# A decoder layer in one written order: transitions, mixer and attention placed by hand per engine

## The chip, the cores and the metric

One core of a Trainium2 chip runs the whole layer in one launch. The metric is device time in microseconds (us). Engines are called TensorE (PE), VectorE (DVE), ScalarE (ACT), GpSimd (POOL) and SyncE (SP, here only a queue that issues transfers).

## The reference

One layer on x of 256 rows by 2048 columns, float32, with a conditioning vector c:

```
mod = silu(c) @ w_ada + b_ada                      # nine rows of 2048
h = modulate(rms_norm(x, g1), mod0, mod1); x += 0.5 * mod2 * swiglu(h)       # FFN 1, width 5632
h = modulate(rms_norm(x, gm), mod3, mod4)
u, q, k, v, ga, gb = split(h @ w_in)               # 1024, 1024, 128, 128, 2048, 2048 columns
y_pool = multiscale_pool(u) @ w_pool_up            # trailing means over 2, 4, 8, 16 rows
y_attn = window_attention(norm(q), norm(k), v, bias, sinks) @ w_attn_up      # 16 heads, window 128
x += mod5 * ((sigmoid(ga) * y_pool + sigmoid(gb) * y_attn) @ w_o)
h = modulate(rms_norm(x, g2), mod6, mod7); x += 0.5 * mod8 * swiglu(h)       # FFN 2
```

## The kernel before

The 256 rows are two tiles t = 0, 1 of 128 partitions. A `Set` multiplies them with a block of up to 1024 weight columns (`SW`) into four of the eight PSUM banks (two t by two chunks of 512 columns, `CW`); the other four banks take transposes and sums. Each weight row block k (128 rows) is split for precision: ScalarE casts the raw weights to `wh` (L300), VectorE subtracts and leaves `wl` (L304); the rows are split the same way into `hh` and `hl` or, for later stages, `sh` and `sl` (L432, L433). `Set.mm` then makes three products: `hh wh` (L316), `hl wh` (L318), `hh wl` (L320), so a full block of k is 12 matmuls of 128x512. Raw weights come by SP's queue into `RAW` = 6 slots of 1 MB.

Two ways of ordering stand side by side:

- FFN 1 and FFN 2 (`ffn`, and the first stage) are under `tc.manual_schedule()`: each engine runs instructions as they are written. `pushes` loads and splits a block and hands its matmuls to `push`, which emits them `LAG` = 2 blocks later, so splits lie two blocks ahead of TensorE. `at(n, f)` hangs any other step behind the matmuls of push n. `spread` places the adaLN sums (one VectorE multiply-add of 128x1024 per row block of `w_ada`, L253) where the planned VectorE time of a push leaves room under `ROOM`; `will` books such time.
- Everything between (both `transition`s, the projection `w_in`, pooling, attention, merge and the first part of the output projection `w_o`) is written in program order through `run`, with hooks after chosen blocks, and a scheduler orders the engines. AdaLN sums go in by a rate (`ada_side`, L182).

A transition: `tail` runs the last four row blocks of the stage that ends, first for t = 0, then t = 1; after each, `residual` (L456, L457) adds gate times result to x, `sumsq` (L371) squares, `rstd` makes the norm's factor, `scaled` (L392) scales 512 columns, `h_T` (L399) transposes them on TensorE, `h_mod` (L409, L411, L413, L414) modulates and splits. The table of position biases (`toeplitz`, L843, L845) is made at the first transition. At the start of FFN 2 `ffn` takes four SiLUs (L542) ahead of its first weights.

The mixer: `qk_norm` hangs in the pooling projection, `pooling` and `heads` (four heads at a time; logits, bias, softmax) in the first two gate stages, `heads_out` (transposes and product with v) later. After each half of the merged rows, eight columns' blocks are transposed by TensorE (`tr`, `pair_T`, L360) into `mT`, the input of `w_o`. In the FFNs the same turn is made without TensorE: `turn_T` transposes 32x32 blocks on VectorE (L521) and 16 ScalarE moves put them in place (L525).

Of the kernel before, what the change touches and what calls it, by code (L numbers as in the profile page):

```python
# [9 lines left out]
F32 = mybir.dt.float32  # L10
# [25 lines left out]
TAIL = 4  # L36
NS = 7
LAG = 2
ROOM = 2.5
# [3 lines left out]
def trunk_layer(ctx, tc, x, c, w_ada, b_ada, g_ffn1, w_ffn1_gu, w_ffn1_down, g_mix, w_in,  # L43
# [50 lines left out]

    late, plan, pushed, done = deque(), {}, [0], [0]
# [23 lines left out]


# [22 lines left out]
    def acc_sum(b, a):  # L143
        w = a.shape[1]
        hi = t_([P, w], "t2", T2, F32R)
        lo = t_([P, w], "t2", T2, F32R)
        nc.scalar.copy(hi, a)
        nc.vector.tensor_tensor(lo, a, hi.bitcast(F32), ALU.subtract)
        nc.tensor.matmul(b, ones, hi, start=True, stop=False)
        nc.tensor.matmul(b, ones, lo, start=False, stop=True)  # L150

# [16 lines left out]
    def ada_item(j, c0, i, a):  # L168

        if i == 0:  # L170
            a.append(t_([P, SW], "acc", 2))
            if j % 3 == 2:
                nc.gpsimd.memset(a[0], 0.0)
                nc.sync.dma_start(a[0][0:1, :], b_ada[0:1, j * D + c0:j * D + c0 + SW])
        raw = t_([P, 2, SW], "raw", RAW)
        nc.sync.dma_start(raw, ada_v[:, 2 * i:2 * i + 2, j * D + c0:j * D + c0 + SW])
        for k in range(2):
            sc = cs[:, 2 * i + k:2 * i + k + 1]
            if i == k == 0 and j % 3 != 2:
                nc.vector.tensor_scalar_mul(a[0], raw[:, k, :], sc)  # L180
            else:
                nc.vector.scalar_tensor_tensor(out=a[0], in0=raw[:, k, :], scalar=sc, in1=a[0],  # L182
                                               op0=ALU.mult, op1=ALU.add)
        if i < 7:
            return
        for o in range(0, SW, CW):
            b = bank()
            acc_sum(b, a[0][:, o:o + CW])
            if j % 3 == 2:
                if j not in gates:  # L190
                    gates[j] = t_([P, D], "gate", 1)
                nc.scalar.activation(gates[j][:, c0 + o:c0 + o + CW], b, AF.Copy, scale=1.0 if j == 5 else 0.5)
            else:
                mod_col(j, b, c0 + o)

    side, sidec = [], [0, 0]

    def ada_side(js, rate):
        sidec[:] = [0, rate]
        for j, c0 in js:  # L200
            a = []
            side.extend(lambda j=j, c0=c0, i=i, a=a: ada_item(j, c0, i, a) for i in range(8))

    def flush():
        while side:
            side.pop(0)()

    def ada_plan(js, n0):


        where = iter(spread(n0, len(js) * KD, 1.28))

        def sums(j, c0, a, n):
            hl_ = []

            def halves(o):
# [3 lines left out]
                hl_[:] = [hi, lo]  # L220

            def use(o):
                b = bank()
                nc.tensor.matmul(b, ones, hl_[0], start=True, stop=False)  # L224
                nc.tensor.matmul(b, ones, hl_[1], start=False, stop=True)  # L225
                if j % 3 == 2:
                    if j not in gates:
                        gates[j] = t_([P, D], "gate", 1)
                    nc.scalar.activation(gates[j][:, c0 + o:c0 + o + CW], b, AF.Copy, scale=1.0 if j == 5 else 0.5)
                else:  # L230
                    mod_col(j, b, c0 + o)

            for i in range(2):
                at(n + 2 * i, lambda i=i: halves(i * CW))
                at(n + 2 * i + 2, lambda i=i: use(i * CW), True)

        for j, c0 in js:
            a, r = [], []
            for kk in range(KD):
                def go(j=j, c0=c0, kk=kk, a=a, r=r):  # L240
                    if kk == 0:
                        a.append(t_([P, SW], "acc", 2))
                        if j % 3 == 2:
                            nc.gpsimd.memset(a[0], 0.0)
                            nc.gpsimd.dma_start(a[0][0:1, :], b_ada[0:1, j * D + c0:j * D + c0 + SW])
                    if kk % 2 == 0:
                        r[:] = [t_([P, 2, SW], "raw", RAW)]
                        nc.sync.dma_start(r[0], ada_v[:, kk:kk + 2, j * D + c0:j * D + c0 + SW])
# [3 lines left out]
                    else:  # L252
                        nc.vector.scalar_tensor_tensor(out=a[0], in0=r[0][:, kk % 2, :], scalar=sc, in1=a[0],  # L253
                                                       op0=ALU.mult, op1=ALU.add)
                n = next(where)
                at(n, go)
            sums(j, c0, a, n + 1)


    class Set:  # L260
# [27 lines left out]

        def prep(self, k, raw_k, extra=False, fine=False, given=None):
            c0, cw = self.cols  # L290
            if given is not None:
                wh, wl = given, t_([P, cw], "wl", 3, F32R)
            elif extra:
                wx = t_([P, 2, cw], "sg", 1, F32R)
                wh, wl = wx[:, 0, :], wx[:, 1, :]
            else:
                wh = t_([P, cw], "wh", 3, F32R)
                wl = t_([P, cw], "wl", 3, F32R)
# [8 lines left out]
        def mm(self, item, t, chunks=None, k0=0, k1=None):  # L307
# [4 lines left out]
            sl = slice(t * P, (t + 1) * P)  # L312
            ch = [(i, slice(*self.chunks[i])) for i in range(len(self.chunks))]
            ch = [(i, slice(o.start, o.start + o.stop)) for i, o in ch if chunks is None or i in chunks]
            for i, o in ch:
                nc.tensor.matmul(self.banks[t][i], hi[:, sl], wh[:, o], start=first, stop=False)  # L316
            for i, o in ch:
                nc.tensor.matmul(self.banks[t][i], lo[:, sl], wh[:, o], start=False, stop=False)  # L318
            for i, o in ch:
                nc.tensor.matmul(self.banks[t][i], hi[:, sl], wl[:, o], start=False, stop=last)  # L320
# [5 lines left out]
        def pushes(self, ka, kb, k0=0, k1=None):  # L326

            grp = min(2 * SW // self.cols[1], 4)
            for a in range(ka, kb, grp):
                raw = self.load(a, min(grp, kb - a))  # L330
                for k in range(a, min(a + grp, kb)):
                    item = self.prep(k, raw[:, k - a, :])
                    push(lambda item=item: [self.mm(item, t, None, k0, k1) for t in range(T)])

        def step(self, k, raw_k, k0=0, k1=None):
            item = self.prep(k, raw_k)
            for t in range(T):
                self.mm(item, t, None, k0, k1)

    def run(s, hooks=None, k0=0, k1=None):  # L340
        grp = min(2 * SW // s.cols[1], 4)
        k1 = s.nk if k1 is None else k1
        for ka in range(k0, k1, grp):
            n = min(grp, k1 - ka)
            raw = s.load(ka, n)
            for k in range(n):
                s.step(ka + k, raw[:, k, :])
                if hooks and (ka + k) in hooks:
                    hooks[ka + k]()
            sidec[0] += sidec[1]  # L350
            while side and sidec[0] >= 1:
                sidec[0] -= 1
                side.pop(0)()
        return s.banks

    def pair_T(src, f0, dst_fn):
        b = bank()
        for f in range(2):
            for t in range(T):
                nc.tensor.transpose(b[:, (2 * f + t) * P:(2 * f + t + 1) * P], src(t, f0 + f), ident)  # L360
        dst_fn(f0, b)
# [40 lines left out]
    def h_mod(b, n, t, jb, hh, hl, fine=False, fs=range(4)):  # L402
        h = t_([P, 4, P], "t2", T2)
        ks = [(f, 4 * n + f) for f in fs]
        d = lambda k, w: (slice(None), slice(k, k + w), slice(t * P, (t + 1) * P))
        for f, k in ks:
            g_, b_, src = mcol[:, jb + 1, k:k + 1], mcol[:, jb, k:k + 1], b[:, f * P:(f + 1) * P]
            if fine and t == 0 and f % 2 == 0:
                nc.vector.tensor_scalar(h[:, f, :], src, g_, b_, ALU.mult, ALU.add)  # L409
            else:  # L410
                nc.scalar.activation(h[:, f, :], src, AF.Identity, scale=g_, bias=b_)  # L411
            if fine:
                nc.scalar.copy(hh[d(k, 1)], h[:, f:f + 1, :])  # L413
                nc.vector.tensor_tensor(hl[d(k, 1)], h[:, f:f + 1, :], hh[d(k, 1)].bitcast(F32), ALU.subtract)  # L414
        if not fine:
            e = d(4 * n, 4)
            nc.scalar.copy(hh[e], h)
            nc.vector.tensor_tensor(hl[e], h, hh[e].bitcast(F32), ALU.subtract)

    def h_tok(n, t, jb, hh, hl):  # L420
        h_mod(h_T(scaled(n, t)), n, t, jb, hh, hl)
# [5 lines left out]
    def split_stat(src, kept=None):  # L427

        cache = {}
# [6 lines left out]
        def stat(k):  # L436
            ka = k - k % 2
            c = cache if kept is None or not 4 <= k < 4 + KD else kept[2]
            if ka not in c:
                n = min(2, src.shape[1] - ka)  # L440
                if c is cache:
# [6 lines left out]

        return stat
# [15 lines left out]
    def tail(s, c0, jgate, after):  # L465

# [652 lines left out]
```

## Time and profile before

| | |
|---|---|
| time, median of 3 (lowest to highest) | 2023.32 us (2020.91 to 2025.42) |
| the profiled execution's own time, its span | 2025.86 us, 2023.8 us |
| TensorE busy, matmuls | 98%, 8889 |
| VectorE, ScalarE busy | 74%, 54% |
| HBM read | 520 MB, 258 GB/s over the span |
| mean granted TensorE clock | 0.996 |

The profile is of one execution. Rows that begin with a line number group instructions: count, busy us, mean ns of one, then the engine's idle time before them and what ended it.

### The profile page before, as it was taken

What the parts mean: (1) busy time and instruction counts of PE and PEld (TensorE: products, weight loads), DVE (VectorE), ACT (ScalarE), POOL (GpSimd) and SP (SyncE); (2) the same over time, 40 slices, a digit from 0 to 9 for tenths busy, and PEclk for the clock granted to TensorE, in tenths of its full rate; (3) what the DMA queues carried; (4) which work ended last, traced back from release to release, by engine and by line L of the source; (5) the groups of instructions that cost most, each with busy time, mean ns of one, the idle gap of its engine ahead of it and who ended that gap; (6) DMA issues with size and microseconds to landing.
All of it is one profiled execution on the core that took longest, in us unless ns stands there. A gap on an engine that the chain in (4) does not pass through costs nothing. (4 is left out here: it accounts for less than half of the span.)

```text
span 2023.8 us, 23691 instructions
## 1 busy us (share of the span) xinstructions
PE 1985.4 (98%) x8889; PEld 1634.4 (81%) x8889; DVE 1494.3 (74%) x1705; ACT 1083.3 (54%) x1473; POOL 15.0 (1%) x32
## 2 busy tenths in 40 slices
PE   7999999999999998999999999999999999999999
PEld 6788888888788886887788887778888888888887
DVE  6888867988999996868788788758755454565655
ACT  5544457665654455546454455644654645565443
POOL 1000000000000000000000000000000000000000
PEclk9999999999999999999999999999999999999999
DMA  9989745899898984777767887458955555466661
GB/s 363 369 304 336 262 154 188 337 351 356 309 344 337 333 332 165 281 266 241 270 234 286 296 287 268 167 190 328 347 195 191 205 187 188 166 227 209 214 198 68
DMA packets 157778, 523.66 MB, mean 259 GB/s; under 512 B 9525, under 2 KB 23518, under 8 KB 157408
## 3 DMA queue, kind: packets, MB, share of 16 engines
q1 hardware_dynamic: 156992, 521.02, 72.2%
q8 instruction: 69, 1.13, 0.2%
q0 software_dynamic: 672, 1.14, 0.1%
q14 instruction: 45, 0.37, 0.0%
HBM read 520.00 MB, written 2.12 MB: 258 GB/s over the span
## 5 line engine op out<-in xcount | busy, mean ns | idle before, releaser
L304 DVE TENSOR_TENSOR wl<-raw,wh 128x1024 fp32r<-128x1024 f32 (+2 forms) x746 | 844.7, 1137 | 423.1 <-ACT wh L300 419.1
L300 ACT CAST wh<-raw 128x1024 fp32r<-128x1024 f32 (+2 forms) x730 | 728.9, 1002 | 784.5 <-PE bank L318 713.5
L316 PE MATMUL bank<-wh,hh 128*128 128x512 f32 x2072 | 655.2, 391 | 7.5 <-ACT hh L413 4.4
L320 PE MATMUL bank<-wl,hh 128*128 128x512 f32 x2072 | 652.6, 390 | 3.5 <-DVE wl L304 3.2
L318 PE MATMUL bank<-wh,hl 128*128 128x512 f32 x2072 | 652.5, 390 | 0.0
L320 PEld LDWEIGHTS bank<-wl,hh 128*128 128x128 f32 x2072 | 390.0, 189 | 87.6 <-DVE wl L304 7.7
L316 PEld LDWEIGHTS bank<-wh,hh 128*128 128x128 f32 x2072 | 389.2, 189 | 88.5 <-ACT hh L413 5.6
L318 PEld LDWEIGHTS bank<-wh,hl 128*128 128x128 f32 x2072 | 390.5, 189 | 82.2 <-DVE hl L414 0.6
L320 PE MATMUL bank<-wl,sh 128*128 128x512 f32 x692 | 216.0, 390 | 1.8 <-DVE wl L304 1.8
L318 PE MATMUL bank<-wh,sl 128*128 128x512 f32 x692 | 216.3, 389 | 0.0
L316 PE MATMUL bank<-wh,sh 128*128 128x512 f32 x692 | 215.7, 390 | 0.0
L253 DVE SCALAR_TENSOR_TENSOR acc<-raw,cs,acc 128x1024 f32<-128x1024 f32 x139 | 177.7, 1278 | 0.3 <-DMA raw<-in_w_ada_dram 0.3
L320 PEld LDWEIGHTS bank<-wl,sh 128*128 128x128 f32 x692 | 129.7, 188 | 29.0 <-DVE wl L304 2.2
L318 PEld LDWEIGHTS bank<-wh,sl 128*128 128x128 f32 x692 | 129.8, 188 | 27.6 <-DVE sl L433 0.6
L316 PEld LDWEIGHTS bank<-wh,sh 128*128 128x128 f32 x692 | 129.6, 188 | 27.7 <-ACT sh L432 0.5
L525 ACT COPY big<-raw 32x512 f32<-32x512 f32 (+1 forms) x192 | 111.9, 583 | 4.0
L182 DVE SCALAR_TENSOR_TENSOR acc<-raw,cs,acc 128x1024 f32<-128x1024 f32 x77 | 98.5, 1279 | 20.1 <-DMA raw<-in_w_ada_dram 19.6
L631 DVE SCALAR_TENSOR_TENSOR acc<-raw,cs,acc 128x1024 f32<-128x1024 f32 (+2 forms) x74 | 77.6, 1050 | 1.6 <-DMA raw<-in_w_ada_dram 0.7
L433 DVE TENSOR_TENSOR sl<-big,sh 128x512 fp32r<-128x512 f32 x88 | 60.2, 684 | 0.0
L432 ACT CAST sh<-big 128x512 fp32r<-128x512 f32 x88 | 54.3, 617 | 9.7 <-DVE big L948 9.7
L738 DVE TENSOR_TENSOR big<-bank,big 128x512 f32<-128x512 f32 x56 | 36.4, 681 | 0.0
L371 ACT ACTIVATE junk<-x_sb 128x512 bf16<-128x512 f32 x24 | 15.1, 630 | 26.3 <-DVE x_sb L457 24.0
(203 smaller groups left out, 713.4 us busy)
## 6 DMA issues: line engine op xcount, KB each, us to landing
raw<-in_w_ffn_gu_dram SPq DMA_DIRECT2D x175, 1024.0 KB, 4.9
raw<-in_w_ada_dram SPq DMA_DIRECT2D x112, 1024.0 KB, 7.6
raw<-in_w_ffn_down_dram SPq DMA_DIRECT2D x88, 1024.0 KB, 5.8
raw<-in_w_in_dram SPq DMA_DIRECT2D x48, 1024.0 KB, 5.3
raw<-in_w_ada_dram SPq DMA_DIRECT2D x64, 512.0 KB, 7.4
raw<-in_w_o_dram SPq DMA_DIRECT2D x16, 1024.0 KB, 6.1
raw<-in_w_pool_up_dram SPq DMA_DIRECT2D x8, 1024.0 KB, 6.1
raw<-in_w_attn_up_dram SPq DMA_DIRECT2D x8, 1024.0 KB, 6.2
```

The lines of the kernel that those rows point to most:

```text
L182: nc.vector.scalar_tensor_tensor(out=a[0], in0=raw[:, k, :], scalar=sc, in1=a[0], op0=ALU.mult, op1=ALU.add)
L253: nc.vector.scalar_tensor_tensor(out=a[0], in0=r[0][:, kk % 2, :], scalar=sc, in1=a[0], op0=ALU.mult, op1=ALU.add)
L300: nc.scalar.copy(wh, raw_k)
L304: nc.vector.tensor_tensor(wl[:, e], raw_k[:, e], wh[:, e].bitcast(F32), ALU.subtract)
L316: nc.tensor.matmul(self.banks[t][i], hi[:, sl], wh[:, o], start=first, stop=False)
L318: nc.tensor.matmul(self.banks[t][i], lo[:, sl], wh[:, o], start=False, stop=False)
L320: nc.tensor.matmul(self.banks[t][i], hi[:, sl], wl[:, o], start=False, stop=last)
L432: nc.scalar.copy(hi, src[:, k:k + n, :])
L433: nc.vector.tensor_tensor(lo, src[:, k:k + n, :], hi.bitcast(F32), ALU.subtract)
L525: nc.scalar.copy(actT[32 * j:32 * j + 32, k:k + m, :].rearrange("p k (t i r) -> p k t i r", t=T, i=4)[:, :, :, i, :], z[0][32 * i:32 * i + ...
L631: nc.vector.scalar_tensor_tensor(out=acc, in0=r, scalar=sc, in1=acc, op0=ALU.mult, op1=ALU.add)
L738: nc.vector.tensor_tensor(a, b, a, ALU.add)
```

## The change

- The whole kernel is under `manual_schedule`; `run`, `step`, `ada_side` and `tail` go, and everything is placed with `at`.
- `transition`: five last blocks (`TA`) instead of four, their splits in slots of their own (`last_items`), and a written interleave: the first residual runs while the second bank is made; h's halves are written directly from the bank by ScalarE (`direct`); the next stage starts with `hh wh` and `hh wl` and adds `hl wh` later; four blocks (`TB`) of it are prepared ahead. The blocks that follow go through `pushes`.
- Mixer: the stages follow each other as pushes (Q, KV, U, then per half: gate a, pool up, gate b, attention up; then `w_o`). QK norm, pooling and attention are cut into steps one push apart; `with_bank` places a TensorE step at a push and its reader at the next (`hop` avoids a stage's last push). Heads go by two, from pushes 3, 7, 10, 14, 17, 21, 25 and 28 of the first gate stage. Each pair loads its bias on SP's queue into one tile.
- The first half of `mT` is turned by `turn_T` (VectorE, ScalarE), the second still by TensorE.
- The bias table's product goes into FFN 1; its loads, the gains and sinks go to POOL's queue, at the start or in FFN 1. Stores of the last half are issued per bank.
- `ROOM` 2.5 to 2.6; adaLN sums: split, product and use in separate pushes; one block of sums in FFN 1 is cut into two of 512 columns.

The core of the diff:

```diff
+    def hop(n, f, g):
+        while n in ends:
+            n += 1
+        at(n, f)
+        at(n + 1, g)
...
     def transition(s, c0, jgate, jb, nxt):
+        flush()
+        hh, hl = new_h()
+        n = nxt(lambda k: (hh[:, k, :], hl[:, k, :]))
+        items = last_items(s, hh, hl)
+        raw = [n.load(k, 2) for k in range(0, TB, 2)]
...
         for i in range(2):
+            for w in items:
+                s.mm(w, 0, (i,))
+        hi(1, "raw"); lo(1); hi(0, "w"); lo(0)
+        res(0, 0); sumsq(0, col); res(0, 1); sumsq(0, col + 1)
+        rstd(0)
+        x00, x10 = scaled(0, 0), scaled(1, 0)
+        for w in items:
+            s.mm(w, 1, (0,))
+        res(1, 0)
+        for w in items[:3]:
+            s.mm(w, 1, (1,))
+        b00, b10 = h_T(x00), h_T(x10)
+        hi(2, "sg"); lo(2)
+        for w in items[3:]:
+            s.mm(w, 1, (1,))
+        hi(3, "w"); lo(3)
+        m00 = h_mod(b00, 0, 0, jb, hh, hl, True, (2, 3))
+        next(m00)
+        sumsq(1, col); res(1, 1); sumsq(1, col + 1)
+        next(m00, None)
+        rstd(1)
+        for w in nx:
+            n.mm(w, 0, order=(0, 2))
...
+    def with_bank(n, shape, f, g):
+        b = []
+        hop(n, lambda: (b.append(bank(shape)), f(b[0])), lambda: g(b[0]))
...
+        at(n - 1, lambda: nc.sync.dma_start(bias, ...))
         for i in range(2):
+            with_bank(n, (P, TOE), logits(i), add(i))
+        do(n + 2, 1.5, top)
+        at(n + 3, exps)
+        do(n + 4, 1.2, over)
+        for i in range(2):
+            with_bank(n + 5, (P, TOE), turn(i), turned(i))
...
+    for g, n in enumerate((3, 7, 10, 14, 17, 21, 25, 28)):
+        heads(G[0] + n, g)
...
+        if half_ == 0:
+            turn_T(lambda sgb=sgb: sgb[0], 0, SW, mT, lambda t: e + 4 + t, lambda q: e + 7 + q // 2)
```

More of the change, by code (lines that the diff above doesn't have):

```diff
@@ L166, in mod_col, with sums, halves @@
             nc.vector.tensor_tensor(m, m, gcol[:, i * KD + k:i * KD + k + n], ALU.mult)
[L168 to L206, printed above, removed]
     def ada_plan(js, n0):
[L211 to L216, printed above, removed]
+        def sums(j, c0, a, n, o):
+            got = []
+            def halves():
                 hi, lo = t_([P, CW], "t2", T2, F32R), t_([P, CW], "t2", T2, F32R)
@@ L219, in halves, with prod, use @@
                 nc.vector.tensor_tensor(lo, a[0][:, o:o + CW], hi.bitcast(F32), ALU.subtract)
[L220 to L225, printed above, removed]
+                got.extend((hi, lo))
+            def prod():
+                got.append(bank())
+                nc.tensor.matmul(got[2], ones, got[0], start=True, stop=False)
+                nc.tensor.matmul(got[2], ones, got[1], start=False, stop=True)
+            def use():
                 if j % 3 == 2:
@@ L252, in go @@
                     else:
-                        nc.vector.scalar_tensor_tensor(out=a[0], in0=r[0][:, kk % 2, :], scalar=sc, in1=a[0],
+                        nc.vector.scalar_tensor_tensor(out=a[0], in0=r[0][:, kk % nk, :], scalar=sc, in1=a[0],
                                                        op0=ALU.mult, op1=ALU.add)
-                n = next(where)
                 at(n, go)
-            sums(j, c0, a, n + 1)
+                will(n, 1.28 * a_w / SW)
+            n0 = n
+            for i in range(a_w // CW):
+                sums(j, c0, a, n + 1 + 2 * i, i * CW)
     class Set:
@@ L312, in mm @@
             sl = slice(t * P, (t + 1) * P)
+            terms = ((hi, wh), (lo, wh), (hi, wl))
             ch = [(i, slice(*self.chunks[i])) for i in range(len(self.chunks))]
             ch = [(i, slice(o.start, o.start + o.stop)) for i, o in ch if chunks is None or i in chunks]
[L315 to L320, printed above, removed]
+            for q in order:
+                a, w = terms[q]
+                for i, o in ch:
+                    nc.tensor.matmul(self.banks[t][i], a[:, sl], w[:, o], start=first and q == 0, stop=last and q == 2)
         def free(self, t, i):
@@ L332, in pushes @@
                     item = self.prep(k, raw[:, k - a, :])
+                    if between is not None and k == ka:
+                        between()
                     push(lambda item=item: [self.mm(item, t, None, k0, k1) for t in range(T)])
[L335 to L361, printed above, removed]
     ssq = const.tile([P, T, 5], F32, name="ssq")
@@ L461, in sqrt_table @@
         nc.scalar.activation(st[:, 6, 0:1], ssq[:, 1, 1:2], AF.Sqrt)
-    def tail(s, c0, jgate, after):
-        items = []
-        for ka in range(s.nk - TAIL, s.nk, 2):
-            raw = s.load(ka, 2)
-            for k in range(2):
-                items.append(s.prep(ka + k, raw[:, k, :], extra=len(items) == TAIL - 1, fine=True))
-        for i in range(2):
-            for it in items:
-                s.mm(it, 0, (i,))
-        residual(s.banks, c0, jgate, after, (0,))
-        yield
-        for i in range(2):
-            for it in items:
-                s.mm(it, 1, (i,))
-        residual(s.banks, c0, jgate, after, (1,), (0,))
-        yield
-        residual(s.banks, c0, jgate, after, (1,), (1,))
@@ L563, in ffn @@
             if sg is None:
-                s = Set(w_gu, KD, (f0, fw), stat, late=True)
-                s.pushes(0, KD)
+                s, g = g or Set(w_gu, KD, (f0, fw), stat, late=True), None
+                s.pushes(TB + LAG if s.banks else 0, KD)
                 sg = t_([P, T, fw], "sg", 1)
@@ L869, in carve @@
         return a.rearrange("p (a b c) -> p a b c", b=shape[1], c=shape[2])
-    def evac(banks, dst):
-        for t in range(T):
-            for i, b in enumerate(banks[t]):
-                w = b.shape[1]
-                nc.scalar.copy(dst[:, t, i * CW:i * CW + w], b)
-    b, hh, hl = transition(s, SW, 2, 3, lambda stat: Set(WI, KD, (QO, PW), stat, flip=False))
-    big = t_([P, KF * S], "big", 1)
     q_sb = carve(0, T, PW)
@@ new lines, in trunk_layer, with pool_prod, f @@
+    with_bank(nU + 11, (P, CW), k_turn,
+              lambda b: nc.scalar.activation(kT.rearrange("p a b -> p (a b)"), b, AF.Copy, scale=gq[:, 1:2]))
+    with_bank(nU + 12, (P, S), v_turn, lambda b: nc.scalar.copy(vR.rearrange("p a b -> p (a b)"), b))
+    pT_ = []
+    def pool_prod(a):
+        def f(b):
+            if not pT_:
+                pT_.append(t_([P, 8, S], "sg", 1))
+            g = a // 2
+            for f_ in range(2):
+                lhs = lambda t: u_sb[:, t, (a + f_) * P:(a + f_ + 1) * P]
+                nc.tensor.matmul(b[:, f_, :], lhs(0), poolw[:, g, 0:S], start=True, stop=False)
+                nc.tensor.matmul(b[:, f_, P:S], lhs(1), poolw[:, g, S:TOE], start=False, stop=True)
+        return f
@@ new lines, in trunk_layer, with pm_load, mix_prod, f @@
+    pm = []
+    def pm_load():
+        pm.append(t_([P, 8, GW], "raw", RAW))
+        nc.sync.dma_start(pm[0], pool_mix[0].rearrange("g (k p) d -> p (g k) d", p=P))
+    def mix_prod(a):
+        def f(b):
+            g, dd = a // 2, a % 2
+            for k in range(2):
+                nc.tensor.matmul(b, pm[0][:, 2 * g + k, dd * P:(dd + 1) * P], pT_[0][:, 2 * g + k, :],
+                                 start=k == 0, stop=k == 1)
+        return f
+    at(nQ + 4, lambda: nc.sync.dma_start(poolw, pool_w.rearrange("g p n -> p g n")))
@@ new lines, in copies, with sig @@
+    def copies(s, dst, e):
+        for t in range(T):
+            for i, (o, w) in enumerate(s.chunks):
+                at(e + t, lambda t=t, i=i, o=o, w=w: nc.scalar.copy(dst[:, t, o:o + w], s.free(t, i)), True)
+    sQ.pushes(TB + LAG, KD)
+    copies(sQ, q_sb, nK - 1)
+    s = Set(WI, KD, (KO, 256), hstat2, late=True)
+    s.pushes(0, KD)
+    copies(s, kv_sb, nU - 1)
+    s = Set(WI, KD, (UO, PW), hstat2, late=True)
+    s.pushes(0, KD)
+    copies(s, u_sb, G[0] - 1)
+    def sig(s, e, dst):
+        for q, (t, i) in enumerate(tk):
+            at(e + q // 2, lambda t=t, i=i: nc.scalar.activation(dst()[:, t, i * CW:(i + 1) * CW], s.free(t, i), AF.Sigmoid), True)
@@ L1049, in trunk_layer @@
+    s = Set(w_o[0], KD, (0, SW), split_stat(mT), late=True)
+    s.pushes(0, KD)
+    for q, (t, i) in enumerate(tk):
+        at(W1 - 1 + 2 * q, lambda t=t, i=i, s=s: (s.free(t, i), residual(s.banks, 0, 5, lambda *a: None, (t,), (i,))), True)
+        at(W1 + 2 * q, lambda t=t, i=i: sumsq(t, i))
+    at(W1 + 8, sqrt_table)
+    s = Set(w_o[0], KD, (SW, SW), split_stat(mT), late=True)
+    s.pushes(0, KD - TA)
     ov = out[0].rearrange("(t p) d -> p t d", p=P)
     def store(t, n):
-        nc.sync.dma_start(ov[:, t, n * CW:(n + 1) * CW], x_sb[:, t, n * CW:(n + 1) * CW])
@@ L1061, in trunk_layer, with end @@
-    for _ in tail(s, SW, 8, store):
-        pass
+    s = ffn(w_ffn2_gu[0], w_ffn2_down[0], hh, hl, actT, 0, None, g, 8, store, [(8, 0, SW), (8, SW, SW)])
+    flush()
+    items = last_items(s, *new_h())
+    def end(t, a, e):
+        o = slice(SW + a, SW + e)
+        y = t_([P, e - a], "t2", T2)
+        nc.vector.tensor_tensor(y, s.banks[t][a // CW][:, a % CW:a % CW + e - a], gates[8][:, o], ALU.mult)
+        nc.vector.tensor_tensor(x_sb[:, t, o], x_sb[:, t, o], y, ALU.add)
+        nc.sync.dma_start(ov[:, t, o], x_sb[:, t, o])
@@ L1065 @@
+    for t in range(T):
+        for i in range(2):
+            for w in items:
+                s.mm(w, t, (i,))
+            end(t, i * CW, (i + 1) * CW)
 _INS = ['x', 'c', 'w_ada', 'b_ada', 'g_ffn1', 'w_ffn1_gu', 'w_ffn1_down', 'g_mix', 'w_in', 'pool_mix',
```

601 lines of the change are left out of this document (350 added, 251 removed).

## The prediction

> **What bounds the kernel now.** I read the page first, for the share of TensorE and the clock; then the busy time by stretches, which tells stages apart; then TensorE's waits stage by stage; last the order of events in the stretch that loses most.
>
> ```profile
> span 2023.8 us, 23691 instructions
> PE 1985.4 (98%) x8889; PEld 1634.4 (81%) x8889; DVE 1494.3 (74%) x1705; ACT 1083.3 (54%) x1473; POOL 15.0 (1%) x32
> ```
>
> TensorE is the bound: busy for 98% of the span. A busy TensorE need not be at its rate, so the second view counts matmuls per stretch (columns: stretch, length, busy time with the number of instructions of PE, weight loads, VectorE, ScalarE, GpSimd; then the granted clock, the DMA share, GB/s).
>
> ```profile
> core 0: us, PE busy (x) PEld busy (x) DVE busy (x) ACT busy (x) POOL busy (x), PEclk, DMA share, GB/s
> 764.00:800.00 36.00, 29.46 (x128) 22.73 (x127) 23.40 (x51) 19.98 (x46) 0.00 (x0) 0.91 0.54 190
> 800.00:1240.00 440.00, 435.47 (x2066) 359.05 (x2065) 346.49 (x450) 225.99 (x345) 1.44 (x2) 1.00 0.77 269
> 1240.00:1280.00 40.00, 38.25 (x168) 30.82 (x167) 33.43 (x46) 23.38 (x33) 1.44 (x2) 1.00 0.64 223
> 1280.00:1360.00 80.00, 76.00 (x337) 60.77 (x336) 48.49 (x71) 47.53 (x84) 0.00 (x0) 0.98 0.46 161
> 1360.00:2000.00 640.00, 640.00 (x2825) 529.81 (x2824) 379.66 (x363) 338.43 (x408) 2.20 (x4) 1.00 0.63 217
> ```
>
> The last row is the second FFN, whose order is written out by hand already: 2825 matmuls in 640.00 us, 0.2266 us each, TensorE never idle. That is the floor for the other stages. 764 to 800 is the first transition (end of FFN 1, norm, start of the projection), 800 to 1240 the mixer, 1240 to 1280 the output projection, 1280 to 1360 the second transition and the start of FFN 2. TensorE's transposes in the two transitions:
>
> ```profile
> L399 PE MATMUL bank<-ident,t 128*128 128x128 f32 x24 | 3.5, 273 | 3.8 <-DVE t L392 3.8
> L399 PE MATMUL bank<-ident,t 128*128 128x128 f32 x32 | 4.8, 277 | 0.4 <-DVE t L392 0.4
> 787.36 1.03 PE L399 MATMUL bank<-ident,t 128*128 128x128 f32 x8
> ```
>
> Eight in a row end after 1.03 us and one lasts 0.273, so one starts every (1.03 - 0.27)/7 = 0.109 us. Transition 1: 36.00 - 104 x 0.2266 - 24 x 0.109 = 9.8 us lost. Transition 2: 80.00 - 305 x 0.2266 - 32 x 0.109 = 7.4 lost. Output projection: 40.00 - 168 x 0.2266 = 1.9 lost. What TensorE waited for, in the three stretches in turn (us in total, times, longest):
>
> ```profile
> PE bank L399 <- DVE t L392: 3.8, 1, 3.8
> PE bank L316 <- ACT hh L413: 2.7, 2, 2.1
> ...
> PE bank L320 <- DVE wl L304: 2.3, 1, 2.3
> PE bank L945 <- DVE big L984: 0.9, 1, 0.9
> PE bank L150 <- DVE t L148: 0.8, 2, 0.6
> PE bank L980 <- ACT sg L973: 0.4, 1, 0.4
> ...
> PE bank L316 <- ACT wh L300: 1.9, 1, 1.9
> PE bank L320 <- DVE wl L304: 1.8, 1, 1.8
> ```
>
> The mixer waits 4.4 us in all. What the waits of the transitions don't cover is the clock:
>
> ```profile
> 777.44:784.26 6.82, 4.74 (x12) 3.67 (x12) 6.08 (x17) 3.24 (x11) 0.00 (x0) 0.50 0.79 275
> 1340.64:1344.05 3.41, 3.41 (x9) 2.64 (x10) 3.30 (x3) 1.67 (x2) 0.00 (x0) 0.50 0.05 12
> ```
>
> After the 3.8 and 2.1 us of idling the clock stands at 0.50 for 6.82 us, and after the single 1.9 us wait for 3.41 us: some 2.4 and 1.7 us of work lost. The Trainium skill (TensorE: Matmul & The Clock Gate, Part 1) puts the halving after an idle window of about 3.4 us; the 1.9 us wait drew it too, so here the measurement decides. By the page's figure short gaps would cost their own length alone.
>
> **The change, part by part.** 1. *Transitions.* Before, the scheduler's order on VectorE between the last t = 0 matmul and the first transposes was:
>
> ```profile
> 767.69 0.55 DVE L845 COPY t<-bank 16x384 f32<-16x384 f32 x1 [2.54 <-PE bank L843]
> 768.17 1.27 DVE L456 TENSOR_TENSOR t<-bank,gate 128x512 f32<-128x512 f32 x2
> 769.36 1.27 DVE L457 TENSOR_TENSOR x_sb<-x_sb,t 128x512 f32<-128x512 f32 x2
> ...
> 773.22 0.15 DVE L387 TENSOR_REDUCE st<-ssq 128x1 f32<-128x5 f32 x1
> ...
> 774.84 0.21 DVE L379 SCALAR_TENSOR_TENSOR st<-st 128x1 f32<-128x1 f32 x1
> ...
> 776.23 0.54 DVE L392 TENSOR_SCALAR t<-x_sb,st 128x512 f32<-128x512 f32 x1
> ```
>
> The position-table copy stood 2.54 us in front of the residual, and splits of weights stood between the statistics' steps: 8.6 us from the residual's start to the end of the scaled row, under 24 matmuls (5.4 us). The new order moves the table into FFN 1, does the first residual while the second bank is still being made, and splits nothing in the chain. What is left after the last t = 0 matmul is one product and one sum (1.27), one square, five small steps (0.15 to 0.21, about 0.9), the scaling (0.54). ScalarE's rows:
>
> ```profile
> L300 ACT CAST wh<-raw 128x1024 fp32r<-128x1024 f32 x177 | 185.4, 1054 | 200.4 <-PE bank L318 186.4 <-DVE wl L304 7.1 <-issue 4.2
> L411 ACT ACTIVATE t<-bank,mcol 128x128 f32<-128x128 f32 x60 | 23.4, 461 | 8.5 <-PE bank L399 8.4
> L300 ACT CAST wh<-raw 128x256 fp32r<-128x256 f32 x16 | 6.5, 408 | 7.9 <-PE bank L318 7.3 <-DVE wl L304 0.5
> L371 ACT ACTIVATE junk<-x_sb 128x512 bf16<-128x512 f32 x12 | 7.6, 630 | 18.6 <-DVE x_sb L457 18.5
> L875 ACT COPY big<-bank 128x512 f32<-128x512 f32 x8 | 4.3, 586 | 1.7 <-PE bank L320 1.7
> L525 ACT COPY big<-raw 32x512 f32<-32x512 f32 (+1 forms) x192 | 111.9, 583 | 4.0
> ```
>
> So 1.27 + 0.63 + 0.9 + 0.54 = 3.3, with some 1 us of hand-overs 4.4 us, under 15 + 9 = 24 matmuls of t = 1, again 5.4 us: the 3.8 us wait goes. Late next: ScalarE writes the halves of h straight from the bank, but two 1.05 us casts stand in front, which wait for slots that matmuls of the last items still read. I put the first h 0.5 us behind the 6 matmuls and 4 transposes that cover it (1.8 us). Then t = 1: product and sum (1.27), two modulated blocks and the split ahead of them on VectorE (about 1.4), statistics 0.9, scaling 0.54, hand-overs 1 = 5.1 us, against 20 matmuls (4.5 us): 0.6 us. With the restart of the pipeline I take 1.5 us per transition. Bounds: 0 (all hidden) and the 7.4 that transition 2 loses today. No gap reaches 1.9 us, so no halved clock. In FFN 2 the four SiLUs came ahead of the first cast (the 1.9 us wait); now they come after the last push, behind casts prepared two ahead: gone.
>
> Five last items instead of four, and all casts ahead of their matmuls: 5 x 1.05 + 2 splits of the stationary rows is 6.5 us of ScalarE, against two items (5.4) and the first items' share of 0.68 each: covered, with about half a microsecond to spare. The same holds at the kernel's end, whose last product, sum and store are as before: 0, bounds -0.5 to +0.5.
>
> 2. *Output projection.* Four residuals that stood together ahead of a split now come one per second push: the 1.9 us goes.
>
> 3. *Mixer.* Pooling, QK norm and attention in small steps, by two heads, each step one push (12 matmuls, 2.72 us) behind the step that feeds it, weights prepared two pushes ahead. Of the 4.4 us of waits (bounds of what is left: 0 and 4.4 plus what VectorE's load brings, below) I leave 1.0, as VectorE is loaded much as in FFN 1. The 0.1 us with which each small group of matmuls enters and leaves stay.
>
> New: the key/value projection has 256 columns, so a push is 6 matmuls of half width, 0.7 us, and two ahead are 1.4. At its start ScalarE empties four banks of q (0.586 each) between casts (0.408): 1.17 + 0.41 before the third push, 1.17 + 0.41 before the fourth, 3.2 us against 2.1: 1.1 us lost (bounds 0 and 3.2).
>
> 4. *Half of mT turned without TensorE.* 16 transposes less, 1.7 us, and 4 bank copies less. VectorE gets two 32x32 block transposes, ScalarE 16 moves of 583 ns, two per push beside a 1.05 us cast: 2.2 of 2.72 us, off the path; with that cover gone it would be 9.3 us.
>
> 5. *Moved issues.* Gains, sinks, bucket table and one-hot go from SP's queue ahead of the projection to POOL's at the start and in FFN 1, behind the seven gain and bias loads that the start needs: 0 (-0.3 to +0.5). The pooling matrices stay on SP but come four pushes into the projection; eight bias loads stay on SP. The adaLN rows are spread with 2.6 instead of 2.5 us of VectorE per push, one sum is cut into two halves of its columns, and sums and their use lie one push further apart: 0, -1 to +2 by FFN 1's waits.
>
> Sum: 9.8 + 7.4 + 1.9 + 4.4 + 1.7 = 25.2 to be had; 2 x 1.5 + 1.1 + 1.0 = 5.1 stays or comes new: 20.1 less. The profiled execution took 2025.86 us (span 2023.8 and 2.1 around it), 2.5 over the median of 2023.32: 2005.8 by its clock, 2003.3 by the median's.
>
> **The rivals.** (a) *Everything is hidden*: neither transition nor projection loses anything: 25 us, 1998, and a microsecond or two more if the small entries shrink. For it: FFN 2's row without a wait. Against it: the tight 0.5 us places above.
>
> (b) *The transitions wait elsewhere.* One late cast or row per transition makes a gap of 2 us; with the 1.7 us that the halved clock took after such a gap, and the 1.5, each costs 5.2: 2010.7. For it: in-order engines, as the 2.54 us in front of the residual show.
>
> (c) *VectorE or the loads become the bound in the mixer.* A push costs VectorE one split and one adaLN row:
>
> ```profile
> L304 DVE TENSOR_TENSOR wl<-raw,wh 128x1024 fp32r<-128x1024 f32 x167 | 202.4, 1221 | 77.5 <-ACT wh L300 77.2
> L182 DVE SCALAR_TENSOR_TENSOR acc<-raw,cs,acc 128x1024 f32<-128x1024 f32 x77 | 98.5, 1279 | 20.1 <-DMA raw<-in_w_ada_dram 19.6
> 440.00:480.00 40.00, 40.00 (x178) 33.06 (x177) 35.89 (x34) 18.96 (x22) 0.00 (x0) 1.00 1.02 394
> ```
>
> 2.50 of 2.72 us, and 2 x 0.524 MB in 2.72 us = 385 GB/s, for the 40 pushes of the second half's gates. The last row shows TensorE at full rate with 394 GB/s and VectorE at 35.89 of 40, so it just holds. If each such push took 0.2 us more, that is 8 us: 2011. The Trainium skill (DMA: Bandwidth & Descriptors, the table at its head) gives 358 GB/s per core from HBM; by it those pushes would take 2.93 us, 8.4 us more, 2012. The 394 GB/s speak against it.
>
> (d) *Slower: SP's single queue.* Each bias load goes into a tile that VectorE's additions of the heads before must have read, and all weight loads queue behind it.
>
> ```profile
> raw<-in_w_in_dram SPq DMA_DIRECT2D x40, 1024.0 KB, 5.3
> SPq L939 <- DVE big L948: 6.3, 4, 3.3
> ```
>
> A weight issued only then lands 5.3 us later and needs a 1.05 us cast. By the written places (heads at pushes 3, 7, 10, 14, 17, 21, 25, 28) the load behind is needed two to three pushes (5.4 to 8.2 us) later, so it is just hidden; VectorE late by a push or more exposes it. Seven waits decide from 20.1/7 = 2.9 us each; at 6.4 each with 1.7 of halved clock they cost 56 less 20: 2060. With half of that, 2031.
>
> **How the numbers follow.** 4 us (0.2%) is about what can be told from no change. Forecast 0.55, its own range 1999 to 2008; (a) 0.11; (b) 0.13; (c) 0.11; (d) 0.10, of which 0.03 falls within 0.2%. All but (d) are faster: 0.90, 0.03, 0.07. The range 1996 to 2014 takes in (a), (b), (c) and leaves out (d) and the worse ends.
>
> **What would show it.** After: no PE wait over 1 us and PEclk 1.00 in both transitions; no wait for a SiLU's cast at FFN 2's start; about 1 us lost where the key/value columns begin; the mixer's waits on wl gone; 16 transposes fewer; VectorE fuller early in the mixer. Wrong would be: gaps over 2 us before h, waits of wl on DMA behind the bias loads, or a VectorE above 95% with TensorE waiting.

## The result, and the profile after

2011.56 us median (2011.42 to 2012.3) against 2022.85 us: 0.9944 of the time before, 95% interval 0.9927 to 0.9961. The profiled execution took 2012.3 us. The changed kernel's page:

```profile
span 2010.5 us, 23739 instructions
PE 1977.7 (98%) x8873; PEld 1629.0 (81%) x8873; DVE 1515.2 (75%) x1759; ACT 1084.2 (54%) x1469; POOL 20.1 (1%) x42
```

TensorE still bounds it, with 16 instructions less and a VectorE that is 21 us fuller. By stretches (the same columns as before):

```profile
764.00:800.00 36.00, 35.63 (x169) 29.31 (x169) 31.04 (x56) 21.08 (x45) 0.00 (x0) 1.00 0.67 246
800.00:1226.00 426.00, 421.52 (x1989) 345.04 (x1988) 354.25 (x492) 226.10 (x348) 2.87 (x4) 1.00 0.77 275
1226.00:1346.00 120.00, 119.74 (x545) 98.92 (x544) 99.20 (x124) 71.34 (x110) 0.00 (x0) 1.00 0.63 230
1346.00:1986.00 640.00, 638.56 (x2817) 528.24 (x2816) 363.77 (x349) 336.39 (x407) 2.19 (x4) 1.00 0.60 208
```

The first row is transition 1, the third the second half of the output projection and transition 2. Without their 24 and 32 transposes, by the floor of 0.2266 us a matmul, 36.00 - 145 x 0.2266 - 24 x 0.109 = 0.5 us are lost in one and 120.00 - 513 x 0.2266 - 32 x 0.109 = 0.3 in the other, where 9.8 and 1.9 + 7.4 were. The clock is 1.00 in both. What TensorE waited for in FFN 1 and after the start, in transition 1, the mixer, transition 2 and FFN 2:

```profile
PE bank L296 <- DVE wl L281: 3.2, 3, 1.8
PE bank L296 <- ACT t L677: 0.6, 1, 0.6
PE bank L296 <- DVE sl L386: 0.3, 1, 0.3
...
PE bank L349 <- DVE t L342: 0.4, 1, 0.4
...
PE bank L296 <- DVE big L1122: 2.7, 1, 2.7
PE bank L296 <- DVE sl L386: 0.6, 1, 0.6
PE bank L1085 <- DVE big L1080: 0.5, 1, 0.5
PE bank L1085 <- DVE big L1122: 0.3, 1, 0.3
...
PE bank L349 <- DVE t L342: 0.3, 1, 0.3
...
PE bank L296 <- ACT gate L199: 1.4, 1, 1.4
```

The mixer kept a wait of 2.7 us, FFN 1 and FFN 2 have new ones. To place the difference I took the start of the same large matmul, counted in order (there are 8352), in both traces; a stage is the time from one such start to the next, and its last matmul's number stands in brackets. In us (in the mixer, where the small matmuls changed places, only the total is comparable):

```
stage                                          before   after-before  f1-before
start, first stage of FFN 1 (200)                81.4       -0.4        -1.9
rest of FFN 1 (3150)                            687.5       +3.1        +3.3
transition 1 and q (3342)                        56.7       -8.9        -8.9
key/value columns (3438)                         13.8       +0.1        +0.1
u, gates, pool up, first attention up (4702)    332.6       +0.7        -6.4
second attention up, w_o, transition 2,
  start of FFN 2 (5620)                         225.5       -9.4        -9.3
next 300 matmuls of FFN 2 (5920)                 70.0       +0.8        -0.4
rest of FFN 2 (8271)                            532.9        0.0         0.0
kernel's end                                     23.4       +0.7        +0.2
```

(f1 is the combined kernel of the experiments.) The transitions gave 18.3 us, more than forecast; the mixer gave nothing and FFN 1 took 3 us back. FFN 1's loss is larger up to its 3100th matmul, 5.1 us; the 50 matmuls after it already run in the new transition's order and give 2.0 back.

### The profile page after: what moved, and what is told of

Same layout as the page of the kernel before. It is cut to its first block, busy times and chain, and to the rows that moved or that the text cites. A ratio compares the mean times of both kernels' runs of the same rounds, so it can differ in the third digit from the quotient of the medians.

```text
span 2010.5 us, 23739 instructions
## 1 busy us (share of the span) xinstructions
PE 1977.7 (98%) x8873; PEld 1629.0 (81%) x8873; DVE 1515.2 (75%) x1759; ACT 1084.2 (54%) x1469; POOL 20.1 (1%) x42
## 4 chain that ended last, share of the span: by engine, by line
PE 89%; DVE 5%; DMA 3%; ACT 1%; issue 1%; SPq 0%; ACTq 0%; DVEq 0%
PE bank L296 86%; DVE wl L281 2%; DMA raw<-in_w_in_dram 1%; DVE acc L223 1%; DMA raw<-in_w_pool_up_dram 1%; ACT wh L277 1%; DMA raw<-in_w_ada_dram 1%; DVE acc L649 0%; PE bank L1024 0%; SPq L641 0%; PE bank L792 0%; DMA raw<-in_w_ffn_down_dram 0%; PE bank L349 0%; PE bank L192 0%; DVE mcol L168 0%
## 5 line engine op out<-in xcount | busy, mean ns | idle before, releaser
L277 ACT CAST wh<-raw 128x1024 fp32r<-128x1024 f32 (+2 forms) x712 | 710.6, 1001 | 805.0 <-PE bank L296 709.8
L281 DVE TENSOR_TENSOR wl<-raw,wh 128x1024 fp32r<-128x1024 f32 (+2 forms) x713 | 822.3, 1156 | 416.5 <-ACT wh L277 409.9
L296 PE MATMUL bank<-wh,hl 128*128 128x512 f32 (+1 forms) x2088 | 654.8, 389 | 0.0
L296 PE MATMUL bank<-wh,hh 128*128 128x512 f32 (+1 forms) x2064 | 651.6, 391 | 2.5 <-ACT gate L199 1.4
L296 PE MATMUL bank<-wl,hh 128*128 128x512 f32 (+1 forms) x2064 | 647.8, 389 | 2.4 <-DVE wl L281 2.3
L223 DVE SCALAR_TENSOR_TENSOR acc<-raw,cs,acc 128x1024 f32<-128x1024 f32 (+1 forms) x231 | 279.4, 1209 | 3.6 <-DMA raw<-in_w_ada_dram 2.8
L296 PE MATMUL bank<-wh,sl 128*128 128x512 f32 x656 | 204.3, 391 | 1.0 <-DVE sl L386 0.9
L296 PE MATMUL bank<-wl,sh 128*128 128x512 f32 x656 | 203.9, 390 | 0.8 <-DVE wl L281 0.8
L187 DVE TENSOR_TENSOR t<-acc,t 128x512 fp32r<-128x512 f32 x28 | 19.2, 687 | 11.2 <-PE bank L192 9.4
L186 ACT CAST t<-acc 128x512 fp32r<-128x512 f32 x28 | 17.3, 617 | 10.3 <-DVE acc L223 10.1
```

The costliest lines, as they stand in the source:

```text
L223: nc.vector.scalar_tensor_tensor(out=a[0], in0=r[0][:, kk % nk, :], scalar=sc, in1=a[0], op0=ALU.mult, op1=ALU.add)
L277: nc.scalar.copy(wh, raw_k)
L281: nc.vector.tensor_tensor(wl[:, e], raw_k[:, e], wh[:, e].bitcast(F32), ALU.subtract)
L296: nc.tensor.matmul(self.banks[t][i], a[:, sl], w[:, o], start=first and q == 0, stop=last and q == 2)
```

## The experiments

### The bias loads on POOL's queue (e1)

```diff
-        at(n - 1, lambda: nc.sync.dma_start(bias, ...
+        at(n - 1, lambda: nc.gpsimd.dma_start(bias, ...
```

> The bias loads of the eight head pairs are issued on POOL's queue instead of SP's; nothing else changes. Theory Q (the single queue): in the changed kernel SP stands 72 us in front of these loads, the weights behind them land late, ScalarE's casts wait 30 us for weights in the mixer, and TensorE pays for it with the 2.9 us gap near 946 us, the 1.7 us of halved clock behind it and some smaller gaps. Then SP's waits for the bias tile go, the casts' waits for weights fall below 15 us, and the time falls by 3 to 7 us. Rival V (VectorE's load): the gaps come from VectorE's steps of the heads themselves, which are late by their own order; then the time moves by less than 1 us.

2006.91 us, 0.9915 (0.9890 to 0.9941). What SP's queue and ScalarE waited for between 800 and 1280 us, in the changed kernel:

```profile
SPq L1095 <- DVE big L1058: 72.2, 7, 13.5
SPq L1095 <- DMA big<-toe: 18.2, 6, 3.7
ACT wh L277 <- DMA raw<-in_w_in_dram: 19.0, 7, 6.6
ACT wh L277 <- DMA raw<-in_w_pool_up_dram: 10.9, 6, 2.8
```

and with the loads on POOL's queue:

```profile
ACT wh L277 <- DMA raw<-in_w_pool_up_dram: 4.2, 3, 2.0
ACT wh L277 <- DMA raw<-in_w_in_dram: 2.9, 2, 1.7
```

The seven waits of 72.2 us are those of the second to eighth pair: VectorE has not yet added the bias of the pair before (L1058), SP stands, and the weights behind it are issued late. For another 18.2 us SP waits for an earlier bias load to land. The casts' waits for weights fall from 29.9 to 7.1 us. Around the worst place TensorE is busy for 57.29 us of 60 before, 60.00 after, and the clock goes from 0.97 to 1.00:

```profile
900.00:960.00 60.00, 57.29 (x276) 45.68 (x276) 38.32 (x84) 34.36 (x73) 0.00 (x0) 0.97 0.47 164
```

```profile
900.00:960.00 60.00, 60.00 (x297) 48.37 (x296) 41.60 (x94) 37.18 (x76) 2.91 (x4) 1.00 0.61 207
```

The mixer stage of the table is 5.7 us shorter than before the change instead of 0.7 longer. Theory Q holds. The whole moved by 4.7 us by the medians, not by these 6.4. In the profiles the start took 1.5 us back: there the halved clock near 68 us lasted 6.83 us in e1, and near 70 us 3.41 in the changed kernel. (One of the four executions took 7089.5 us, the others 2006.8 to 2007.0; its cause is open, and the three kernels below with the same edit had no such one.)

### The smaller budget (e2)

```diff
-ROOM = 2.6
+ROOM = 2.5
```

> ROOM is 2.5 again instead of 2.6, so that the adaLN sums are spread a little thinner. Theory R (the larger budget overfills VectorE in FFN 1): the 5.1 us that FFN 1 lost between its 1400th and 3100th matmul against the kernel before falls to 1 us or less, the time by 4 to 5 us less whatever the mixer gives back. Rival S (the place of the sums: split, product and use now lie closer to the half-width stage): FFN 1 stays within 1 us of its 5.1 us loss, the time moves by less than 1 us.

2018.35 us, 0.9970 (0.9960 to 0.9980): 6.8 us slower by the medians. Between the 1400th and the 3100th matmul FFN 1 loses 2.4 us against the kernel before instead of 5.1: the larger budget is about half of that loss, less than theory R asks for and more than its rival allows, so neither holds. But the next 50 matmuls, where FFN 1 ends, take 7.5 us longer than in the changed kernel. VectorE at the end of FFN 1:

```profile
757.54 0.69 DVE L187 TENSOR_TENSOR t<-acc,t 128x512 fp32r<-128x512 f32 x1 [0.69 <-ACT t L186]
761.62 0.69 DVE L165 TENSOR_TENSOR t<-bank,ident 128x512 f32<-128x512 f32 x1 [3.39 <-PE bank L193]
762.35 0.69 DVE L168 TENSOR_REDUCE mcol<-t 128x4 f32<-128x512 f32 x1
...
763.34 1.22 DVE L435 TENSOR_TENSOR wl<-raw,wh 128x1024 fp32r<-128x1024 f32 x1
```

With the thinner spread the last sum ends with FFN 1, its use stands in front of the last blocks' splits, and VectorE idles 3.39 us for its product. TensorE then waits 2.6 us for the first split and 1.0 for one of the rows, and from 765.22 us on its clock is halved for 6.83 us. So the larger budget costs time inside FFN 1 and saves more at its end.

### The small loads at the start (e3, e6)

```diff
-    nc.gpsimd.dma_start(rel[0:NB, :], rel_bias)     # with sinks, q and k gains: ahead of all work
+    small()                                          # e3: in program order at FFN 1's last part
+    at(pushed[0] + 4, small)                         # e6: four pushes in, with the one-hot
-    hop(pushed[0] + 8, toe_prod, toe_out)
+    hop(pushed[0] + 14, toe_prod, toe_out)           # e6
```

> The loads of the bias table's buckets, the sinks and the q and k gains go from POOL's queue at the start to POOL's queue in FFN 1, beside the one-hot. Theory L (the small loads delay the first weights): the first large matmul starts 1.9 us earlier, at 25.5 us. By the halved clock that follows, either 1.9 us reach the end or, if the clock's window is then twice as long as in the kernel before (6.8 instead of 3.4 us at half), next to nothing: time 0 to 2 us less. Rival: the small loads don't matter and the first large matmul stays at 27.4 us.

> The bucket table, the one-hot, the sinks and the gains are loaded four pushes into FFN 1's last part, behind a sum's first load on POOL's queue, so that POOL cannot run ahead to them; the table's product moves six pushes on. In the run before, POOL had nothing to wait for and issued them at the start all the same. Theory L (the small loads delay the first weights): the first large matmul starts at 25.5 us instead of 27.3. Time 0 to 2 us less, by the length of the halved clock near 68 us (3.4 or 6.8 us). Rival: the start is later for another reason, and stays at 27.3 us.

e3 measured 2014.15 us, and its first large matmul stayed at 27.4 us: POOL had nothing to wait for and issued the loads at the start all the same, so it tested nothing. e6 measured 2013.54, with the first large matmul at 25.6. TensorE's waits for weights at the start and the third of them, in the changed kernel and in e6:

```profile
PE bank L701 <- DMA raw<-in_w_ada_dram: 3.5, 3, 1.7
14.55 1.01 PE L701 MATMUL bank<-cs,raw 128*128 128x1 f32 x4 [1.29 <-DMA raw<-in_w_ada_dram]
```

```profile
PE bank L696 <- DMA raw<-in_w_ada_dram: 1.4, 3, 0.5
13.68 1.01 PE L696 MATMUL bank<-cs,raw 128*128 128x1 f32 x4 [0.49 <-DMA raw<-in_w_ada_dram]
```

Theory L holds: the small loads delay the first weights by 1.8 us. Most of it seems to belong to the sinks and the four gains: e7 below, which adds only the buckets (2 KB) and the one-hot (49.5 KB) to the start of the kernel before, has its first large matmul only 0.3 us later than that kernel. That split was not tried in the changed kernel. e6 as a whole lost the gain again: its table's product, six pushes later, met a stage's end, with a 1.9 us wait near 391 us and a halved clock of 3.41 us; and a second halved clock of 3.41 us came at 516.73 us, behind a 1.8 us wait that the changed kernel has too, without one. In the changed kernel the late start cost little, since the halved clock near 70 us lasted 3.41 us instead of the 6.83 before.

### The use of a sum at a stage's end (e4)

```diff
-            hop(n + 2, prod, use)
+            n += 2
+            while n in ends or n + 1 in ends:
+                n += 1
+            at(n, prod)
+            at(n + 1, use)
```

> A sum's product is no longer placed in the last push but one of a stage, so that its use does not fall into the last push, right ahead of the stage that takes the bank. Theory U: the 1.4 us wait of TensorE for the gate copy near 1415 us in FFN 2 goes, the time falls by 1.5 us. Rival: the copy only comes late because of the SiLUs in front of it, and the wait moves elsewhere: less than 0.5 us.

2014.44 us, 0.9951 (0.9933 to 0.9969). The edit moves two products, one in the mixer and one in FFN 2; in FFN 1 all stay where they were. In FFN 2 the 1.4 us wait is gone and the stage is 1.2 us shorter, as theory U has it. In the mixer the product moves into the first half's attention up, where another stands already: that stage grew by 2.6 us (0.45 of it are the product's two matmuls), and the second half's pool up by 1.0. The 1.0 us that FFN 1 grew by cannot come from the edit. So the rule helps in FFN 2 only.

### The turn of the merged rows (e5, e9)

```diff
-        if half_ == 0:
+        if False:                       # both halves by pair_T; e5 drops the booked time too, e9 keeps it
             turn_T(...)
```

> The first half of the merged rows is turned by TensorE again (16 transposes and 4 bank copies at two pushes), in the changed kernel's order; the block transposes and the 16 moves go. By the prediction the turn without TensorE saves 16 x 0.109 = 1.7 us: then the stage of the second half's first gate grows by 1.5 to 2 us, and the other stages stay. Rival: VectorE's two block transposes and ScalarE's moves cost as much in that stage as the transposes; then it grows by less than 0.5 us or shrinks.

> As the turn by TensorE before, but the VectorE time that was booked for the block transposes stays booked, so that the adaLN sums lie where the changed kernel has them. Theory P (the 3.9 us that the output projection lost then came from sums that moved into its first pushes, not from the turn): the output projection is back within 0.3 us of the changed kernel, the second half's first gate stays 1.5 to 2 us longer, and the whole is 2 to 4 us slower than the changed kernel. Rival: the transposes themselves hold TensorE up there, and the 3.9 us stay.

e5 2019.19 us, e9 2014.08. The second half's first gate is 1.9 us longer in both (1.7 by the prediction's count). Right behind it e5 has a wait of 1.7 us for a sum's use (L165), which e9 has not. e5's output projection is 4.0 us longer, e9's not at all: that was an adaLN product which the planner, with more room, put where its bank still held a merged block:

```profile
PE bank L192 <- DVE sg L1186: 2.8, 1, 2.8
```

Theory P holds. In e9 FFN 1 is 1.2 us longer than in the changed kernel, though its order is the same: a difference of that size in a stage of one profile shows nothing.

### Two parts alone, in the kernel before (e7, e8)

```diff
+    at(pushed[0] + 8, toe_prod); at(pushed[0] + 9, toe_out)      # e7: bias table in FFN 1
...
-            silus(sg, lambda t, i: g[t][i])
+            at(pushed[0], lambda sg=sg: silus(sg, lambda t, i: g[t][i]))      # e8
```

> The kernel before, with one part of the change: the table of position biases is made in FFN 1, so that its product and copy no longer stand in the first transition. Prediction's step: the copy stood 2.54 us in front of the residual. Theory T1 (this alone makes the first transition late): the stage from the end of FFN 1 to the projection falls by 2.5 to 5 us of the 8.9 us that the change saves there, and the halved clock goes. Rival: the splits between the statistics' steps fill the time as well; it falls by less than 1.5 us, and the gain needs the whole written order.

> The kernel before, with one part of the change: at the start of FFN 2 the four SiLUs come behind the first push, so that the first three casts stand ahead of them on ScalarE. Theory: the 1.9 us wait of TensorE for the cast near 1338 us goes and with it the halved clock of 3.4 us: 3 to 3.6 us less in that stage and in all. Rival: the SiLUs then hold up the casts that follow or the sums' banks, and less than 1 us is left of it.

e7: 2021.64 us, 0.9994 (0.9981 to 1.0007), not to be told from before. Transition 1 is 1.4 us shorter of 8.9, and its waits are

```profile
PE bank L316 <- ACT hh L413: 2.7, 2, 2.1
PE bank L399 <- DVE t L392: 2.3, 1, 2.3
```

The 3.8 us wait fell to 2.3, the 2.7 stayed, and so did the halved clock of 6.83 us. Theory T1 fell, and its rival's bound of 1.5 us held. The other cause that the prediction names is the splits that the scheduler puts between the statistics' steps; that these are the rest was not tried alone.

e8: 2021.08 us, 0.9986 (0.9975 to 0.9997). The start of FFN 2 is 3.8 us shorter, the 1.9 us wait and its halved clock are gone, as expected. The output projection took 3.1 us of it back: its wait for a split, 1.8 us before, is 3.2 here, and the clock is halved for 3.41 us behind it, though nothing was changed there:

```profile
PE bank L320 <- DVE wl L304: 3.2, 1, 3.2
```

### Combined (f1, f2, f3)

f1: e1; e6 with the table's product at push 8; e4 in FFN 2 alone. f2: also the two sums of a block three pushes apart in FFN 1. f3: f1 with product and use in one push in FFN 1.

```diff
-            for i in range(a_w // CW):
-                sums(j, c0, a, n + 1 + 2 * i, i * CW)
+                sums(j, c0, a, n + 1 + 3 * i, i * CW)                  # f2, FFN 1
...
+                at(n, lambda: (prod(), use()), True)                   # f3, FFN 1
```

> The changed kernel with three edits: bias loads on POOL's queue; the small loads four pushes into FFN 1's last part, with the table's product where it was; in FFN 2 alone a sum's product not in the last push but one. By the single runs: 4.8 to 5.5 us for the bias loads, 1.8 at the start and 1.3 of halved clock there, 1.2 to 1.6 in FFN 2: 2002 to 2003 us. Rival: POOL's queue, which now carries both the bias loads and the small loads, holds one up behind the other: more than 2005.

> The same, and in FFN 1 the two sums of a block lie three pushes apart instead of two. Theory B (two uses of 1.7 us each come one push after the other in the half-width stage and hold VectorE's splits up: 2.7 us near 510 us): that wait goes, and FFN 1 is 1.5 to 3 us shorter: 2000 to 2001 us. Rival: the place only moves the collision to another push; FFN 1 within 0.7 us of the other.

> The combined kernel, and in FFN 1 a sum's product and its use stand in one push again, ahead of the push's other steps, as in the kernel before. Theory H (the use one push later, the change's hop, is what lengthens FFN 1): FFN 1 is 2 to 3 us shorter, 407.7 to 409 us between its 1400th and 3150th matmul instead of 410.9, the whole 1999.5 to 2000.5. Rival: the larger budget and the block cut in two, which stay, are what lengthens it: FFN 1 within 0.7 us of 410.9.

f1: 2002.35 us (1999.75 to 2004.03), 0.9888 (0.9873 to 0.9902), as expected. f2: 2001.22, 0.9882 (0.9865 to 0.9898); the 1.8 us wait near 510 us is split into three of at most 0.7, but FFN 1 is 410.5 us from its 1400th to its 3150th matmul against f1's 410.9: theory B fell. f3: 2006.2, 0.9915 (0.9898 to 0.9932); FFN 1 410.2: theory H fell too, and the mixer lost 3 us at a product that waits for its bank (2.8 us, and a halved clock of 3.41 us behind it). Both f1 and f2 beat the changed kernel; they cannot be told from each other. f1's waits from 100 to 2000 us:

```profile
PE bank L300 <- DVE wl L285: 3.2, 3, 1.8
PE bank L300 <- DVE sl L390: 1.0, 2, 0.6
PE bank L300 <- ACT t L676: 0.6, 1, 0.6
PE bank L353 <- DVE t L346: 0.6, 2, 0.3
PE bank L193 <- DVE t L187: 0.3, 1, 0.3
```

## Why the prediction was right or wrong

The direction was right and the transitions gave what was forecast of them; the size was not right: 11.3 us came by the medians, 20.1 were forecast, and 2011.56 us lies outside the sum's own range of 1999 to 2008. It lies in the wide range, near the prices of the rivals (b) and (c), 2010.7 and 2011, but neither of these happened; that is luck.

- *Transitions*: forecast 9.8 - 1.5 and 1.9 + 7.4 - 1.5, together 16.1; the stages gave 18.3. The first row of h came under its cover without a wait, where 0.5 us were taken, and the transposes of t = 1 waited 0.4 and 0.3 us, where 0.6 were. No halved clock, as forecast. Of the two causes that the prediction names in transition 1, the copy in front of the residual was the smaller part (e7: 1.4 of 8.9); the rest came with the whole order, and no run takes it apart. The SiLUs' share is shown by e8.
- *Key/value columns*: 1.1 us forecast, 0.1 measured. The hand-over of q's banks was covered; this term of the sum was mis-sized.
- *Mixer without them*: -5.1 forecast (4.4 and 1.7 to be had, 1.0 left), +0.7 measured. The step that failed is rival (d)'s condition: the prediction held the loads behind the bias to be just hidden. They were not, and the sign that it named for that, waits on DMA behind the bias loads, is there (29.9 us of ScalarE's casts). 6.4 us of this stage are SP's queue (e1), and with the loads on another queue the stage gives 5.7, near the sum. The rival's mechanism was right and its price, 2.9 us for each of seven waits to decide, was not reached: 6.4 us over seven waits are 0.9 each, though SP stood for up to 13.5. Why so little of that reached TensorE no run shows.
- *The turn*: 1.7 us forecast, 1.9 in the stage beside it.
- *Moved issues and planning*: forecast 0, -1 to +2. Measured: 1.8 us at the start (small loads), +3.1 in FFN 1, beyond the bound, and +0.8 in FFN 2 (-0.4 with e4's edit). FFN 1's loss is settled only in part: of the 5.1 us up to its 3100th matmul the larger budget is 2.7 (e2). The distance of the sums (f2) and the later use (f3) move it by no more than 0.7, which one profile cannot tell from nothing; the block cut in two was not tried alone.
- *The kernel's end*: forecast 0, -0.5 to +0.5. It is 0.7 us longer in the changed kernel's profile, behind the last matmul, and 0.2 in f1's; the cause is open.
- *VectorE or the loads as the bound (c)*: the 40 pushes with 385 GB/s wanted (the second half's gates and pool up) take 0.8 us less than before. They hold 16 transposes less (1.7 us) and four product matmuls more (4 x 0.2266 = 0.9 us), so nothing was lost there: not the bound. The Trainium skill (DMA: Bandwidth & Descriptors, the table at its head) gives 358 GB/s per core from HBM, by which the prediction's estimate was 8.4 us more there. No such loss shows.

## What to carry to other kernels

In a written order a queue is an engine like any other: a load that waits for a reader must not stand on the queue that carries the weights (e1). A load without a wait ran at once, however late it was written (e3); to move it, put it behind something that waits. And when a planner's budget is changed, look first at what ends last in its stretch: in e2 the leftover landed in front of the next stage's first steps.

## What the runs showed of the hardware

Small transfers beside the first weights cost 1.8 us of lateness: five of 0.2 to 8 KB, one of 2 KB and one of 49.5 KB, of which the last two alone cost 0.3 us in another kernel (e7).

What draws a halved clock, and for how long, was not found. The same 1.5 us wait near 66 us was followed by 6.83 us at half (before, e1), by 3.41 (changed kernel) and by none (e6, e7). A wait of 2.8 us was followed by 3.41 us at half in f3 and by none in e5's output projection; the mixer's 2.3 us wait in the kernel before drew none, while its 1.9 us wait at FFN 2's start drew 3.41. So half of 3.41 or of 6.83 us, 1.7 or 3.4, of difference between two profiles can come without a cause that the order of the work shows.
